# Pooling mixer, first channel group: pool the normed input before the modulation, scale afterwards, add the shift times a pooled row of ones

## The chip, the cores and the metric

The kernel runs on one core of one Trainium2 chip. The metric is the device time of one execution in microseconds (us); each figure is the median of several executions. The core has a matrix engine (TensorE, PE in the rows), a vector engine (VectorE, DVE), an activation engine (ScalarE, ACT), a general engine (GpSimd, POOL), and a queue (SyncE, SP) from which all loads of this kernel are issued. Each engine takes its instructions in the order in which the built program lists them.

## The reference, cut to what matters

Two layers of a diffusion trunk. In layer 0 the token mixer is a centred average pool over time, in four channel groups of 512 channels with windows 2, 4, 8 and 16, followed by a 512x512 product per group. It is computed for a latent stream of 256 tokens and a context stream of 256 tokens.

```python
a_lat = modulate(rms_norm(h, norm1_g[i]), ml[:, 0], ml[:, 1])   # x * (1 + scale) + shift
...
cs = jnp.cumsum(jnp.pad(ug, ((0, 0), (left + 1, right), (0, 0))), axis=1)
window_sum = cs[:, win:win + T] - cs[:, :T]
parts.append(window_sum / count[None, :, None] - ug)            # pooled minus itself
...
y = jnp.einsum('btgc,gcd->btgd', p, w).reshape(B, T, D) + b
h = h + ml[:, 2] * y_lat
```

The shift and the scale are one number per channel and come out of `silu(c) @ w_mod`. Pooling runs over time, so a scale per channel can be put on before or after it, and a shift per channel contributes the shift times what pooling makes of a row of ones.

## The kernel before, in words

Channels lie on the 128 partitions, and the two streams lie beside each other in the free axis, so a channel block of 128 is a 128x512 tile (s = 0 latent, s = 1 context). The residual is kept as `hl` and `hc`.

- `mod_pe(0, ch, ...)` (L187) computes 512 of the 12288 modulation numbers: 4 MB of `w_mod` in eight loads `wm` of 512 KB, 16 products on a quarter of the array each (L193, tile `mod`), a copy out of PSUM on ACT (L198, `modev`), four transposes on PE (L203, `modt`), and a few tiny DVE instructions that leave `modT`. It yields four times. Numbers 0 to 3 are the shift for the four groups, 4 to 7 the scale, 8 to 11 the gate, 12 to 15 the next shift, 16 to 19 the next scale. `mods()` lists them, and `need(n)` runs that list up to step n.
- `mixer(g)` (L413) handles one channel group in steps between yields. For each of its four channel blocks DVE multiplies the residual by scale and norm (`py`, L426), ACT adds the shift into a padded tile (`pad`, L428), DVE adds the window (`ws`, L434), POOL multiplies by one over the count (`pf`, L439), DVE takes off the input (L440), and `pf` is split into a high and a low part (`ph`, L442 on ACT, L443 on DVE), since a 32-bit product is done as three products. The weights `wp` are split alike (`wp0h` on ACT L142, `wp0l` on DVE L144). Then 48 products (`pm`, L457 to L459) go into four PSUM banks one after the other, each bank is read by ACT with the gate (`pz`, L464), added to the residual on POOL (L466) and squared for the next norm (`n2q`, L249). At last the updated residual times the next scale is split into `Ad` (L475, L476).
- `partial(g, ...)` multiplies `Ad` with the first blocks of the feed-forward weights (`wcg`, `wcu` split by L142 and L144; products `cg`, `cu`, L518 to L520), while the modulation loads go on.

The text of the program is not the order that runs: the builder schedules the instructions by a model of its own and fixes an order per engine. `lend` names the tiles of a pool that loads may use as room besides six of their own, so it sets how many loads can be ahead: 18 tiles of 512 KB in the first stretch.

Of the kernel before, what the change touches and what calls it, by code (L numbers as in the profile page):

```python
# [17 lines left out]
P = 128  # L18
D = 2048
KT = D // P  # L20
T = 256
# [36 lines left out]
def kernel(ctx: ExitStack, tc: tile.TileContext, xT, cxT, wmod, wg, wu, wd, wp,  # L58
# [237 lines left out]
    with ExitStack() as ph0:  # L296
# [62 lines left out]
        with ExitStack() as phs:  # L359
# [32 lines left out]
            def mods():  # L392

                for g in range(4):
                    for w in (0, 1, 2, 4):
                        yield from mod_pe(0, 4 * w + g, sc, f0)
                    yield from mod_pe(0, 12 + g, sc, f0)
                    shifts(g)
# [13 lines left out]

            def mixer(g):  # L413
# [7 lines left out]
                for i in range(4):  # L421
# [7 lines left out]
                    src, w = pad, 1  # L429
                    while w < win:  # L430
                        n = WP - 2 * w + 1
                        if w == 1:
                            dst = st.tile([P, 2, WP], F32, tag="ws", name=f"ws{k}")
                        nc.vector.tensor_tensor(dst[:, :, :n], src[:, :, :n], src[:, :, w : w + n], op=ALU.add)  # L434
                        src, w = dst, 2 * w
                    o = PAD - win // 2
                    pf = f0.tile([P, 2, T], F32, tag="t2", name=f"pf{k}")
                    for s in both:
                        nc.gpsimd.tensor_tensor(pf[:, s, :], src[:, s, o : o + T], inv_t, op=ALU.mult)  # L439
                    nc.vector.tensor_tensor(pf, pf, pad[:, :, PAD : PAD + T], op=ALU.subtract)  # L440
                    ph = ap0.tile([P, 2, 2, T], F32R, tag=f"A{k}", name=f"ph{k}")
                    nc.scalar.copy(ph[:, 0], pf)  # L442
                    nc.vector.tensor_tensor(ph[:, 1], pf, ph[:, 0].bitcast(F32), op=ALU.subtract)  # L443
                    pa.append(ph)
# [6 lines left out]
                for m in range(4):  # L451
                    ps = bank("d", f"pm{g}_{m}")
                    for i in range(4):
                        hi, lo = parts[i // 2]
                        c = 512 * (i % 2) + P * m
                        rh, rl = flat(pa[i][:, 0]), flat(pa[i][:, 1])
                        nc.tensor.matmul(ps, hi[:, c : c + P], rh, start=(i == 0), stop=False)  # L457
                        nc.tensor.matmul(ps, hi[:, c : c + P], rl, start=False, stop=False)
                        nc.tensor.matmul(ps, lo[:, c : c + P], rh, start=False, stop=(i == 3))  # L459
# [83 lines left out]
            lend(range(4, KT))  # L543
# [635 lines left out]
```

## Time and profile before

| | |
|---|---|
| median of 3 runs | 3152.26 us (3151.38 to 3156.24) |
| the profiled execution | 3144.81 us, of which the span of the instructions is 3143.0 us |
| PE busy | 3047.0 us of the span |
| DVE, ACT, POOL busy | 2034.4, 1366.9, 938.9 us |
| first product of the mixer | 57.32 us after the span's start |
| first product of the feed-forward part | 79.08 us |

Times in the rows below count from the span's start. A row of the timeline gives start, duration, engine, line of the code, operation, the tile written and the tiles read, shapes and how many instructions it merges; in brackets stands how long the engine was idle before it and who ended the wait. Matmul durations overlap, so what one costs is the distance of the starts.

### The profile page before, as it was taken

What the parts mean: (1) busy time and instruction counts of PE and PEld (TensorE: products, weight loads), DVE (VectorE), ACT (ScalarE), POOL (GpSimd) and SP (SyncE); (2) the same over time, 40 slices, a digit from 0 to 9 for tenths busy, and PEclk for the clock granted to TensorE, in tenths of its full rate; (3) what the DMA queues carried; (4) which work ended last, traced back from release to release, by engine and by line L of the source; (5) the groups of instructions that cost most, each with busy time, mean ns of one, the idle gap of its engine ahead of it and who ended that gap; (6) DMA issues with size and microseconds to landing.
All of it is one profiled execution on the core that took longest, in us unless ns stands there. A gap on an engine that the chain in (4) does not pass through costs nothing.

```text
span 3143.0 us, 40920 instructions
## 1 busy us (share of the span) xinstructions
PE 3047.0 (97%) x15082; PEld 2415.6 (77%) x15082; DVE 2034.4 (65%) x2854; ACT 1366.9 (43%) x2219; POOL 938.9 (30%) x845
## 2 busy tenths in 40 slices
PE   6999999999999999999999999999999999999998
PEld 2565568887877778787778787878778888888887
DVE  4345664387586776868676665564767666666666
ACT  4333454323233232333334444343545665556665
POOL 2011213304132140403223000000002476667776
PEclk9999999999999999999999999999999999999999
DMA  9878663375554646556463333333345555555553
GB/s 380 332 269 315 207 210 101 105 231 182 171 195 158 203 160 198 182 174 195 163 214 115 101 115 105 104 110 97 111 146 183 174 183 201 187 185 179 180 187 116
DMA packets 161545, 559.72 MB, mean 178 GB/s; under 512 B 17600, under 2 KB 22208, under 8 KB 161344
## 3 DMA queue, kind: packets, MB, share of 16 engines
q1 hardware_dynamic: 161344, 557.10, 53.1%
q8 instruction: 119, 1.95, 0.2%
q14 instruction: 82, 0.67, 0.1%
HBM read 554.93 MB, written 2.10 MB: 177 GB/s over the span
## 4 chain that ended last, share of the span: by engine, by line
PE 73%; DVE 11%; DMA 9%; issue 3%; POOL 2%; ACT 1%; SPq 0%; DVEq 0%; POOLq 0%; ACTq 0%
DMA wm<-wmod 9%; DVE macc L221 6%; PE g L731 5%; PE u L731 5%; PE d L776 4%; PE mod L193 3%; PE d L627 3%; PE d L625 3%; PE d L626 3%; PE g L732 3%; PE u L732 2%; PE d L777 2%; PE u L602 2%; PE u L603 2%; PE u L601 2%
## 5 line engine op out<-in xcount | busy, mean ns | idle before, releaser
L221 DVE SCALAR_TENSOR_TENSOR macc<-wm,sc,macc 128x512 f32<-128x512 f32 x480 | 411.0, 880 | 222.8 <-DMA wm<-wmod 218.3
L638 POOL TENSOR_TENSOR hl<-hl,dy 128x256 f32<-128x256 f32 x160 | 160.2, 1001 | 937.3 <-ACT dy L637 936.3
L788 POOL TENSOR_TENSOR hl<-hl,dy 128x256 f32<-128x256 f32 x320 | 320.3, 1034 | 45.4 <-ACT dy L786 43.8
L637 ACT ACTIVATE dy<-d,modT 128x256 f32<-128x256 f32 x320 | 133.3, 470 | 172.9 <-PE d L627 167.3
L638 POOL TENSOR_TENSOR hc<-hc,dy 128x256 f32<-128x256 f32 x160 | 180.0, 1125 | 0.0
L193 PE MATMUL mod<-wm,sc 128*32 128x512 f32 x768 | 133.8, 619 | 24.4 <-DMA wm<-wmod 24.4
L344 ACT ACTIVATE sg<-g 128x512 f32<-128x512 f32 x43 | 27.2, 631 | 295.3 <-DVE g L341 295.3
L875 POOL TENSOR_TENSOR rk<-rk,rp 128x256 f32<-128x256 f32 x16 | 13.8, 862 | 366.1 <-DVE rk L874 302.4
L786 ACT ACTIVATE dy<-d,modT 128x512 f32<-128x512 f32 x160 | 103.6, 686 | 29.7 <-PE d L777 28.3
L439 POOL TENSOR_TENSOR pf<-ws,inv 128x256 f32<-128x256 f32 x32 | 28.4, 907 | 220.4 <-DVE ws L434 152.1
L144 DVE TENSOR_TENSOR wd_2l<-wd,wd_2h 128x1024 fp32r<-128x1024 f32 (+1 forms) x44 | 57.0, 1301 | 48.4 <-ACT wd_2h L142 47.6
L755 DVE TENSOR_TENSOR actb<-sgb,actb 128x256 fp32r<-128x256 f32 x43 | 71.9, 1671 | 21.5 <-ACT actb L754 20.3
L193 PEld LDWEIGHTS mod<-wm,sc 128*32 128x32 f32 x768 | 23.5, 110 | 78.7 <-issue 61.5
L627 PE MATMUL d<-act,wd_0l 128*128 128x512 f32 x172 | 71.1, 414 | 12.3 <-DVE wd_0l L144 12.3
L144 DVE TENSOR_TENSOR wd_0l<-wd,wd_0h 128x1024 fp32r<-128x1024 f32 (+1 forms) x44 | 54.2, 1234 | 34.3 <-ACT wd_0h L142 33.6
L142 ACT CAST wd_0h<-wd 128x1024 fp32r<-128x1024 f32 (+1 forms) x44 | 45.2, 1031 | 67.5 <-PE g L602 36.1
L961 ACT ACTIVATE sb<-sb,nm 128x512 f32<-128x512 f32 x64 | 46.2, 722 | 63.1 <-DVE nm L957 61.4
L625 PE MATMUL d<-act,wd_0h 128*128 128x512 f32 x172 | 70.1, 408 | 0.0
L626 PE MATMUL d<-act,wd_0h 128*128 128x512 f32 x172 | 69.8, 406 | 0.0
L627 PE MATMUL d<-act,wd_1l 128*128 128x512 f32 x172 | 68.0, 396 | 0.1
L626 PE MATMUL d<-act,wd_2h 128*128 128x512 f32 x172 | 68.0, 395 | 0.0
L625 PE MATMUL d<-act,wd_3h 128*128 128x512 f32 x172 | 68.0, 395 | 0.0
(1754 smaller groups left out, 10054.0 us busy)
## 6 DMA issues: line engine op xcount, KB each, us to landing
wm<-wmod SPq DMA_DIRECT2D x384, 512.0 KB, 5.1
wd<-wd SPq DMA_DIRECT2D x168, 512.0 KB, 4.5
wg<-wg SPq DMA_DIRECT2D x156, 512.0 KB, 4.1
wu<-wu SPq DMA_DIRECT2D x156, 512.0 KB, 4.8
wv<-wv SPq DMA_DIRECT2D x32, 512.0 KB, 3.8
wk<-wq SPq DMA_DIRECT2D x32, 512.0 KB, 3.7
wq<-wq SPq DMA_DIRECT2D x32, 512.0 KB, 3.7
wo<-wo SPq DMA_DIRECT2D x32, 512.0 KB, 3.7
```

Of the source, the lines that this page charges most:

```text
L144: eng.tensor_tensor(lo[:, :n], t[:, :n], hi[:, :n].bitcast(F32), op=ALU.subtract)
L193: nc.tensor.matmul(ps[32 * j : 32 * j + 32, :], sc[:, 4 * g + j, :], ts[j // 2][0][:, 512 * (j % 2) : 512 * (j % 2) + 512], start=(g == 0) ...
L221: nc.vector.scalar_tensor_tensor(acc[s], w, sc2[:, k, s : s + 1], acc[s], op0=ALU.mult, op1=ALU.add)
L625: nc.tensor.matmul(ps, hi[:, o : o + P], xh, start=(i == 0), stop=False)
L626: nc.tensor.matmul(ps, hi[:, o : o + P], xl, start=False, stop=False)
L627: nc.tensor.matmul(ps, lo[:, o : o + P], xh, start=False, stop=(i == n - 1))
L637: nc.scalar.activation(y[:, s], ps[:, T * s : T * s + T], AF.Copy, scale=M(0, 5, k, s))
L638: nc.gpsimd.tensor_tensor(h_of(s)[:, k, :], h_of(s)[:, k, :], y[:, s], op=ALU.add)
L731: nc.tensor.matmul(ps, hi[:, c : c + P], flat(B[k]), start=(k == 0), stop=False)
L732: nc.tensor.matmul(ps[:, T:], lo[:, c : c + P], B[k][:, 0], start=False, stop=(k == KT - 1))
L776: nc.tensor.matmul(ps, hi[:, o : o + P], flat(acts[i]), start=(i == 0), stop=False)
L788: nc.gpsimd.tensor_tensor(hl[:, k, :], hl[:, k, :], y[:, q], op=ALU.add)
```

## The change

For group 0 alone, `mixer` works in another order. It multiplies the residual by the norm only (L468, on DVE) into the padded tiles, pools these (`windows`, `pooled`), and keeps the four results `pf` in a room of the pool that loads used before. A row `z` is made from ones in the same way. When the modulation is there, ACT scales each `pf` in place (L478), DVE adds shift times `z` (L479), and the split follows. The weights `wp0` are asked for after eight instead of eleven modulation steps, the scale is computed before the shift, the 48 products run with the channel block outside and the four banks inside (all four banks open at once), and loads have 15 rooms in the first stretch instead of 18. Groups 1 to 3 keep their instructions.

```diff
@@ mods()
-                    for w in (0, 1, 2, 4):
+                    for w in (0, 1, 2, 4) if g else (1, 0, 2, 4):
                         yield from mod_pe(0, 4 * w + g, sc, f0)
@@
+            def windows(pad, win, name):
...
+            def pooled(pf, pad, inv_t, win, name):
+                src, o = windows(pad, win, name)
+                for s in both:
+                    nc.gpsimd.tensor_tensor(pf[:, s, :], src[:, s, o : o + T], inv_t, op=ALU.mult)
+                nc.vector.tensor_tensor(pf, pf, pad[:, :, PAD : PAD + T], op=ALU.subtract)
@@ mixer(g)
+                if g == 0:
+                    z = ap0.tile([P, 1024], F32, tag="A6", name="z")[:, 0:T]
+                    one = pads[1][:, 0:1]
+                    nc.gpsimd.memset(one[:, :, PAD : PAD + T], 1.0)
+                    src, o = windows(one, win, "wz")
+                    nc.vector.tensor_tensor(z, src[:, 0, o : o + T], inv_t, op=ALU.mult)
+                    nc.vector.tensor_scalar(z, z, -1.0, None, op0=ALU.add)
+                    pfs = []
+                    for k in range(4):
...
+                        for s in both:
+                            nc.vector.tensor_tensor(pad[:, s, PAD : PAD + T], h_of(s)[:, k, :], rs1[:, T * s : T * s + T],
+                                                    op=ALU.mult)
+                        pfs.append(room[:, k % 2])
+                        pooled(pfs[k], pad, inv_t, win, f"ws{k}")
+                    yield
+                    parts = ld(wp[0], "wp0")
+                    yield
+                    for k in range(4):
+                        for s in both:
+                            v = pfs[k][:, s, :]
+                            nc.scalar.activation(v, v, AF.Copy, scale=M(0, 1, k, s))
+                            nc.vector.scalar_tensor_tensor(v, z, M(0, 0, k, s), v, op0=ALU.mult, op1=ALU.add)
+                        pa.append(parts_of(pfs[k], k))
+                    yield
+                    banks = [bank("gu", f"pm0_{m}") for m in range(4)]
+                    for i in range(4):
+                        for m in range(4):
+                            pool_mm(banks[m], parts, pa, i, m)
@@ the driver
-            lend(range(4, KT))
+            lend(range(7, KT))
             mix = mixer(0)
-            for n in STEPS:
-                need(n + 2)
+            for n in (0, 8, 11, 15, 15, 19, 19):
+                need(n)
                 next(mix)
```

The built orders show what the scheduler makes of it. First ACT, after the copy of the first norm (`rs`). Before, from there to the first split of a pooled block; `modev_0` and `modev_4` are the shift and the scale of group 0:

```order
L369 COPY rs_194<-n1b 128x512
L198 COPY modev_0_239<-mod_0_206 128x512
L198 COPY modev_4_282<-mod_4_249 128x512
L428 ACTIVATE pad_198<-py_322,modT_0_246 128x256 x2
L428 ACTIVATE pad_200<-py_336,modT_0_246 128x256 x2
L442 CAST ph_333<-pf_329 128x512
```

Now, the same stretch of ACT:

```order
L369 COPY rs_194<-n1b 128x512
L198 COPY modev_4_279<-mod_4_246 128x512
L478 ACTIVATE pf_216<-pf_216,modT_4_286 128x256 x4
L478 ACTIVATE pf_231<-pf_231,modT_4_286 128x256 x4
L198 COPY modev_0_323<-mod_0_290 128x512
L142 CAST wp0h_329<-wp_0_325 128x1024
L142 CAST wp0h_333<-wp_1024_327 128x1024
L433 CAST ph_374<-pf_216 128x512
```

The second modulation copy now stands behind the scaling of all four pooled blocks, and the weight split stands behind that copy.

Second, PE around the mixer's first products. Before, the modulation products of number 8 stand together, ahead of the mixer:

```order
L193 MATMUL mod_8_293<-wm_8_2_0_310,sc 32x512 x2
L193 MATMUL mod_8_293<-wm_8_2_1024_312,sc 32x512 x2
L193 MATMUL mod_8_293<-wm_8_3_0_390,sc 32x512 x2
L193 MATMUL mod_8_293<-wm_8_3_1024_392,sc 32x512 x2
L203 MATMUL modt_8_400<-ident,modev_8_398 128x128 x4
L193 MATMUL mod_16_408<-wm_16_0_0_409,sc 32x512 x2
L457 MATMUL pm_0_435<-ph_333,wp0h_382 128x512
```

Now, the middle of the mixer's products:

```order
L442 MATMUL pm_1_442<-ph_381,wp0h_329 128x512
L193 MATMUL mod_8_345<-wm_8_2_0_362,sc 32x512 x2
L443 MATMUL pm_1_442<-ph_381,wp0l_330 128x512
L442 MATMUL pm_2_443<-ph_381,wp0h_329 128x512
L443 MATMUL pm_2_443<-ph_381,wp0l_330 128x512
L442 MATMUL pm_3_444<-ph_381,wp0h_329 128x512
L443 MATMUL pm_3_444<-ph_381,wp0l_330 128x512
L193 MATMUL mod_8_345<-wm_8_2_1024_364,sc 32x512 x2
L441 MATMUL pm_0_441<-ph_388,wp0h_333 128x512
```

The last four loads of number 8 are now multiplied one by one between mixer products, and the transposes `modt_8` stand behind all 48 of these.

Third, ACT from the last bank of group 0 to the first feed-forward weights. Before:

```order
L464 ACTIVATE pz_514<-pm_3_501,gbi_321,gsc_320 128x256 x2
L249 ACTIVATE n2q_519<-hl 128x256
L198 COPY modev_16_531<-mod_16_408 128x512
L249 ACTIVATE n2q_519<-hc 128x256
L142 CAST wcg_0h_591<-wcg_0_0_587 128x1024
L475 ACTIVATE Ad_567<-hl,modT_16_538 128x256
L475 ACTIVATE Ad_567<-hc,modT_16_538 128x256
```

Now:

```order
L514 ACTIVATE pz_522<-pm_3_444,gbi_209,gsc_208 128x256 x2
L249 ACTIVATE n2q_518<-hc 128x256
L249 ACTIVATE n2q_527<-hl 128x256
L198 COPY modev_16_539<-mod_16_416 128x512
L249 ACTIVATE n2q_527<-hc 128x256
L525 ACTIVATE Ad_575<-hl,modT_16_546 128x256
...
L525 ACTIVATE Ad_590<-hc,modT_16_546 128x256
L142 CAST wcg_0h_599<-wcg_0_0_595 128x1024
```

The split of the first feed-forward weights moved from ahead of the eight `Ad` to behind them.

## Rows read from the trace of the kernel before

**Rows 1.** First part of the page: busy time, share of the span, instructions.
```profile
PE 3047.0 (97%) x15082; PEld 2415.6 (77%) x15082; DVE 2034.4 (65%) x2854; ACT 1366.9 (43%) x2219; POOL 938.9 (30%) x845
```

**Rows 2.** Busy time by stretch: engines in turn, granted clock, DMA share, GB/s.
```profile
40.00:60.00 20.00, 13.54 (x56) 4.38 (x57) 16.31 (x29) 9.03 (x16) 6.72 (x8) 0.91 1.03 408
60.00:80.00 20.00, 18.55 (x98) 9.11 (x97) 6.62 (x14) 11.31 (x25) 5.69 (x8) 1.00 1.00 385
...
51.00:55.00 4.00, 2.85 (x8) 0.18 (x4) 4.00 (x6) 2.74 (x5) 1.54 (x2) 0.57 1.03 409
...
80.00:220.00 140.00, 139.90 (x786) 84.24 (x785) 52.60 (x93) 48.16 (x82) 12.91 (x16) 1.00 0.83 300
220.00:436.00 216.00, 214.31 (x1145) 123.66 (x1144) 148.19 (x258) 93.73 (x174) 48.67 (x45) 1.00 0.77 268
```

**Rows 3.** Timeline of PE, from the second modulation to the feed-forward products.
```profile
40.38 0.66 PE L203 MATMUL modt<-ident,modev 128*128 128x128 f32 x4 [0.69 <-ACT modev L198]
...
50.65 3.20 PE L193 MATMUL mod<-wm,sc 128*32 128x512 f32 x8 [2.79 <-DMA wm<-wmod]
...
72.73 0.39 PE L458 MATMUL pm<-ph,wp0h 128*128 128x512 f32 x1
72.95 0.39 PE L459 MATMUL pm<-ph,wp0l 128*128 128x512 f32 x1
...
79.08 0.73 PE L518 MATMUL cg<-Ad,wcg_0h 128*128 128x512 f32 x2
```

**Rows 4.** Timeline of PE: modulation products in a row, and alone between others.
```profile
76.37 2.78 PE L193 MATMUL mod<-wm,sc 128*32 128x512 f32 x24
...
80.81 0.39 PE L518 MATMUL cg<-Ad,wcg_0h 128*128 128x512 f32 x1
81.13 1.05 PE L193 MATMUL mod<-wm,sc 128*32 128x512 f32 x4
...
82.45 0.39 PE L520 MATMUL cg<-Ad,wcg_0l 128*128 128x512 f32 x1
```

**Rows 5.** Timeline of ACT in the first 80 us.
```profile
31.30 0.59 ACT L369 COPY rs<-n1b 128x512 f32<-128x512 f32 x1 [11.01 <-PE n1b L272]
...
39.74 0.59 ACT L198 COPY modev<-mod 128x512 f32<-128x512 f32 x1 [6.80 <-PE mod L193]
42.36 0.91 ACT L428 ACTIVATE pad<-py,modT 128x256 f32<-128x256 f32 x2 [2.03 <-DVE py L426]
...
52.54 1.03 ACT L142 CAST wp0h<-wp 128x1024 fp32r<-128x1024 f32 x1
...
64.41 1.02 ACT L464 ACTIVATE pz<-pm,gbi,gsc 128x256 f32<-128x256 f32 x2 [5.00 <-PE pm L459]
65.81 0.42 ACT L249 ACTIVATE n2q<-hl 128x256 f32<-128x256 f32 x1 [0.38 <-POOL hl L466]
...
77.31 0.51 ACT L475 ACTIVATE Ad<-hl,modT 128x256 fp32r<-128x256 f32 x1 [0.33 <-DVE modT L183]
77.73 0.49 ACT L475 ACTIVATE Ad<-hc,modT 128x256 fp32r<-128x256 f32 x1
```

**Rows 6.** Timeline of DVE in the first 80 us.
```profile
43.30 0.72 DVE L434 TENSOR_TENSOR ws<-pad 128x542 f32<-128x542 f32 x1 [0.64 <-ACT pad L428]
...
45.73 0.69 DVE L440 TENSOR_TENSOR pf<-pf,pad 128x512 f32<-128x512 f32 x1 [0.53 <-POOL pf L439]
...
52.74 1.22 DVE L144 TENSOR_TENSOR wp0l<-wp,wp0h 128x1024 fp32r<-128x1024 f32 x1
...
78.33 0.48 DVE L476 SCALAR_TENSOR_TENSOR Ad<-hl,modT,Ad 128x256 fp32r<-128x256 f32 x1
78.73 0.48 DVE L476 SCALAR_TENSOR_TENSOR Ad<-hc,modT,Ad 128x256 fp32r<-128x256 f32 x1
```

**Rows 7.** Timeline of POOL in the first 80 us.
```profile
44.16 1.54 POOL L439 TENSOR_TENSOR pf<-ws,inv 128x256 f32<-128x256 f32 x2 [16.49 <-DVE ws L434]
47.20 1.80 POOL L439 TENSOR_TENSOR pf<-ws,inv 128x256 f32<-128x256 f32 x2 [1.50 <-DVE ws L434]
```

More of the change, by code (lines that the diff above doesn't have):

```diff
@@ L411, with parts_of, pool_mm @@
             STEPS = (9, 9, 9, 9, 13, 13, 17, 17)
+            def windows(pad, win, name):
+                src, w = pad, 1
+                while w < win:
+                    n = WP - 2 * w + 1
+                    if w == 1:
+                        dst = st.tile([P, 2, WP], F32, tag="ws", name=name)[:, 0 : pad.shape[1]]
+                    nc.vector.tensor_tensor(dst[:, :, :n], src[:, :, :n], src[:, :, w : w + n], op=ALU.add)
+                    src, w = dst, 2 * w
+                return src, PAD - win // 2
+            def pooled(pf, pad, inv_t, win, name):
[3 more added lines that the diff above has]
+                nc.vector.tensor_tensor(pf, pf, pad[:, :, PAD : PAD + T], op=ALU.subtract)
+            def parts_of(pf, k):
+                ph = ap0.tile([P, 2, 2, T], F32R, tag=f"A{k}", name=f"ph{k}")
+                nc.scalar.copy(ph[:, 0], pf)
+                nc.vector.tensor_tensor(ph[:, 1], pf, ph[:, 0].bitcast(F32), op=ALU.subtract)
+                return ph
+            def pool_mm(ps, parts, pa, i, m):
+                hi, lo = parts[i // 2]
+                c = 512 * (i % 2) + P * m
+                rh, rl = flat(pa[i][:, 0]), flat(pa[i][:, 1])
+                nc.tensor.matmul(ps, hi[:, c : c + P], rh, start=(i == 0), stop=False)
+                nc.tensor.matmul(ps, hi[:, c : c + P], rl, start=False, stop=False)
+                nc.tensor.matmul(ps, lo[:, c : c + P], rh, start=False, stop=(i == 3))
             def mixer(g):
@@ L420, in mixer @@
                 pa = []
-                for i in range(4):
+                banks = []
+                if g == 0:
[7 more added lines that the diff above has]
+                    for k in range(4):
+                        if k % 2 == 0:
+                            room = ap0.tile([P, 2, 2, T], F32, tag=f"A{4 + k // 2}", name=f"pf{k}")
+                        pad = pads[k % 2]
+                        for s in both:
[17 more added lines that the diff above has]
+                            pool_mm(banks[m], parts, pa, i, m)
+                for i in range(4 if g else 0):
                     k = 4 * g + i
@@ L428, in mixer @@
                         nc.scalar.activation(pad[:, s, PAD : PAD + T], y[:, s], AF.Identity, bias=M(0, 0, k, s))
[L429 to L436, printed above, removed]
-                    pf = f0.tile([P, 2, T], F32, tag="t2", name=f"pf{k}")
[L438 to L444, printed above, removed]
+                    pf = f0.tile([P, 2, T], F32, tag="t2", name=f"pf{k}")
+                    pooled(pf, pad, inv_t, win, f"ws{k}")
+                    pa.append(parts_of(pf, k))
                     if i == 3:
@@ L451, in mixer @@
                 for m in range(4):
[L452 to L459, printed above, removed]
+                    if banks:
+                        ps = banks[m]
+                    else:
+                        ps = bank("d", f"pm{g}_{m}")
+                        for i in range(4):
+                            pool_mm(ps, parts, pa, i, m)
                     k = 4 * g + m
```

## The prediction

> **What bounds the kernel now.** I read the page's busy times first: PE is busy for 97% of the span [rows 1], so a change can win only where PE waits, and loses wherever it gives PE more to do. Then the stretches around the first mixer group [rows 2]. From 40 to 60 us PE is busy for 13.54 us and from 60 to 80 us for 18.55 us, so it waits 7.9 us in all; the loads run at 408 and 385 GB/s meanwhile, at full share. From 80 us on there is nothing left to win: 139.90 us busy of 140, then 214.31 of 216. So whatever the change does has to show in the instant at which the first feed-forward product starts, 79.08 us [rows 3], and in the PE work behind it. Last the timeline of PE [rows 3]: one wait of 2.79 us at 50.65 us is for a load, and the products behind it take 3.20 us because the granted clock is down (0.57 on average from 51 to 55 us [rows 2], which is the lower level, 1.2 GHz, for most of it). That cost 0.43 x 4 = 1.7 us of full speed. The most that the edit can win on the way to 79.08 us is thus 7.9 + 1.7 = 9.6 us, 0.3% of the time. About 0.2%, 6.3 us, is what a measurement of this kernel can tell from no change.
>
> **The change, first part: the way to the first feed-forward product.** I follow the new orders with durations from the rows; the clock of the trace of before is the scale.
>
> 1. The copy of the first norm ends at 31.30 + 0.59 = 31.9 us [rows 5]. Now 128 KB of counts are loaded ahead of the weights (0.3 us at 408 GB/s) and two small instructions for the row of ones stand in DVE's chain ahead of the norm. I add 0.4 us: 32.3.
> 2. DVE's four multiplies at 0.40 us a start (the nearest row is the `Ad` pair, 78.33 to 78.73 [rows 6]) and a window addition of 0.7 [rows 6]: 34.6. POOL then needs 1.54 to 1.80 us for a block [rows 7], say 1.65: 36.3 for the first, 38.0 for the second. The two padded tiles are used twice, so the third block waits for the subtraction from the second (0.65, as DVE's 0.69 row overlaps a little [rows 6]) and its own window addition: POOL runs it from 39.4 to 41.1 and the fourth to 42.8; its subtraction ends at 43.5.
> 3. ACT scales the fourth block in two instructions, 0.9 [rows 5]: 44.4. Only then may it copy the shift out of PSUM, which before began at 39.74 [rows 5]: it ends at 45.0 instead of 40.3. PE's transposes (0.66 [rows 3]) stand next on PE, so PE waits for them, and they end at 45.7.
> 4. ACT's two weight splits stand behind that copy (1.03 each [rows 5]): 46.0 and 47.0. DVE takes the first low part (1.22 [rows 6]) to 47.2, the tiny shift instructions to 47.6, the second low part to 48.7, eight additions of shift times row at 0.40 to 51.95, the first low part of a block to 52.6. The first mixer products (high parts) run at about 50, seven us earlier than the 57.3 us of before.
> 5. From 52.6 on PE is the pace. 44 of the 48 products are left, at 0.228 each (72.73 to 72.95 [rows 3]): 10.0. Four lone modulation loads stand among them. Of these one costs 1.64 - 2 x 0.228 = 1.18 us (80.81 to 82.45 with one product and the run between [rows 4]), against 2.78 for six loads in a row, or three pairs [rows 4]: 4.7. That is 67.3. The clock may be low at this point, as after the wait at 50.65; I take half of the 1.7 us: 68.2.
> 6. Now the part that overlapped before: the four banks finish together, and the gate's transposes stand behind all 48 products. Transposes 0.6 and four tiny DVE instructions: 69.7. From the read of a bank to the square of its residual 1.4 us go by (64.41 to 65.81 [rows 5]), and the next bank's read stands behind that square (0.34 more), so a bank takes 1.74 and four take 7.0: 76.7. Then the copy of number 16 (0.6), its transposes (0.65), DVE (0.6): 78.55. In the meantime PE has nothing but four more pairs of loads, and waits some 4 us.
> 7. Eight `Ad` on ACT at 0.41 a start [rows 5]: 81.9. The split of the first feed-forward weights stands behind them now: high part 82.9, low part 84.1. Four products go ahead of the low part (0.9), so PE is where it would be with a start at 83.2.
>
> Before, that start was 79.08. The first part costs **4.1 us**: pooling does begin earlier, but ACT's order holds back the shift, and the evictions that lay under products before lie bare. The unknown prices: the multiply of residual by norm has no row, between 0.35 (DVE's additions, scaled by their length) and 0.48 each; the clock term between 0 and 1.7 for one gap, with up to three gaps (at 46, 52 and 73 to 77 us); POOL between 1.54 and 1.80. Together -2 to +4 us around the 4.1.
>
> The rooms: load n now waits for the release of load n - 15. By the release times above the 42nd load, the second half of the first feed-forward weights, can be issued at about 70 us and is needed after 84; cover of more than 10 us, so nothing for it, and 1 us if that cover were gone. The scratch instructions on DVE and POOL before 31 us are in step 1. Memsets lie in the first 5 us, where DVE and POOL have no other work.
>
> **Second part: modulation products between others.** The scheduler, set off by another start, arranges the rest of the head anew. Counted in PE's order from the first feed-forward product to the last modulation product, the 308 modulation products stand in 76 runs before and in 83 now. A run costs 0.86 us for each four products begun (76.37 to 79.08 for 24 instructions, which are twelve products: 2.71 = 3 x 0.86 + 0.13 [rows 3, 4]) and 0.32 us for going in and out (1.18 - 0.86). The begun fours grow from 102 to 106. So PE gets 7 x 0.32 + 4 x 0.86 = **5.6 us** more work, in a stretch in which it waited 1.8 us of 356 [rows 2]. Bounds: nothing, if the new arrangement fills waits that I don't see; 7, if the new crossings to the short transposes cost as much.
>
> The other engines: DVE is busy 52.60 of 140 and 148.19 of 216 us there [rows 2], and gets nothing new; the later groups keep their instructions.
>
> **The sum.** 4.1 + 5.6 = 9.7 us. The profiled execution took 3144.81 us and would take 3154.5. The median is 7.5 us above that execution, so on the median: 3152.3 + 9.7 = **3162.0 us**, +0.31%.
>
> **The rivals.**
> - *Only the first part counts.* The seven extra runs fill waits of PE. For it: schedulers place loose work where they see a wait. Against it: 1.8 us of waits in 356 us [rows 2]. It gives 3152.3 + 4.1 = 3156.4 us, no change that can be told.
> - *The waits of PE are filled, and it isn't slower.* Pooled blocks are ready when the shift comes, so PE goes through 40 to 79 us without a wait. For it: the long chain from modulation to first product, 40.4 to 57.3 us, is just what the edit takes apart. Against it: the three places of ACT's order above. Its price is the whole 9.6 us, so with the second part 3152.3 - 9.6 + 5.6 = 3148.3. It decides as soon as the first feed-forward product comes before 79.8 us, since then first and second part stay under 6.3 us together.
> - *The clock falls and stays low.* The new order has three gaps of 3 to 5 us on PE before 80 us, where before had one of 2.79 us that lowered the clock [rows 2, 3]. If each costs the full 1.7 us on the path, the sum grows by 3 x 1.7 - 0.85 = 4.2 us: 3166 us. The Trainium skill, in "TensorE: Matmul & The Clock Gate", part 1 on the clock gate, has the half clock as the state to which the array goes back whenever it has been idle for a while, and which only sustained work ends; by it every one of the three gaps would be paid for. The trace agrees at its one gap (0.57 granted).
>
> **How the numbers follow.** Both parts as summed: 0.5. Only the first part: 0.2. The waits filled: 0.2. The clock: 0.1. The first is the forecast, 3162 us. The range must take in the cases on both sides: from 3150, which keeps the upper part of the case with filled waits, to 3168, a little above the clock's case. Within the first case alone it is 3157 to 3166. Slower by over 0.2%: most of the first and all of the last, 0.57. Faster by over 0.2% needs filled waits and a second part near nothing: 0.06. The same: 0.37.
>
> **What would show it.** In the profile after: the copy of the shift at about 44 us, behind the scaling; first mixer products near 50, the last near 68; a PE wait of 4 us between 70 and 78; the first feed-forward product at 83. Then PE busy without a wait to 440 us, with the last modulation product some 10 us later than before. The prediction is wrong if pooling is done before 40 us, if the evictions overlap, or if the modulation products between 80 and 440 us take no more PE time than before.

## The result, and the profile after

Over 20 executions each, the changed kernel took a median of 3159.95 us (3152.95 to 3169.00) and the kernel before 3150.62 us (3142.39 to 3156.24). The ratio is 1.0032, with a 95% interval of 1.0023 to 1.0040: 9.3 us slower, where 9.7 were forecast. The forecast of 3162.0 us lies 2.0 us above the measured median; 1.6 of these are the baseline, since the prediction had the median of three executions of the kernel before (3152.26) and this is the median of 20. The profiled execution of the changed kernel took 3169.00 us, the longest of its 20, over a span of 3167.2 us. So 24 us between the two profiles is more than the change did; which part of it belongs to the change is read below from places in the program.

First the page's busy times:

```profile
PE 3058.2 (97%) x15082; PEld 2419.7 (76%) x15082; DVE 2031.6 (64%) x2865; ACT 1364.5 (43%) x2219; POOL 940.3 (30%) x846
```

Then the same stretches as in [rows 2] (busy time and count of PE, PEld, DVE, ACT, POOL, then granted clock, DMA share, GB/s):

```profile
40.00:60.00 20.00, 12.67 (x47) 6.22 (x48) 10.81 (x20) 6.65 (x11) 2.38 (x3) 0.66 1.03 408
60.00:80.00 20.00, 14.93 (x82) 7.06 (x85) 4.08 (x9) 7.81 (x18) 6.63 (x8) 0.97 0.86 305
80.00:100.00 20.00, 17.98 (x105) 9.12 (x97) 7.71 (x17) 8.48 (x15) 0.00 (x0) 0.95 0.95 335
100.00:220.00 120.00, 120.00 (x658) 70.14 (x662) 47.42 (x83) 41.12 (x72) 13.12 (x16) 1.00 0.80 292
220.00:436.00 216.00, 213.31 (x1134) 123.66 (x1127) 135.62 (x239) 85.53 (x160) 42.10 (x43) 0.99 0.73 254
```

PE has as many instructions as in [rows 1] and is busy for 11.2 us more. In the first two stretches it is busy for 0.87 and 3.62 us less than in [rows 2], so it waits 12.4 us there where it waited 7.9. The waits did not go; they grew.

The timeline of PE shows the places. In the changed kernel L441 to L443 are the mixer's products, and L568 to L570 are the first feed-forward products:

```profile
45.22 1.12 PE L203 MATMUL modt<-ident,modev 128*128 128x128 f32 x4 [5.78 <-ACT modev L198]
46.27 1.94 PE L193 MATMUL mod<-wm,sc 128*32 128x512 f32 x8
50.31 2.07 PE L441 MATMUL pm<-ph,wp0h 128*128 128x512 f32 x4 [2.11 <-ACT ph L433]
52.32 1.94 PE L193 MATMUL mod<-wm,sc 128*32 128x512 f32 x8
54.18 0.74 PE L442 MATMUL pm<-ph,wp0h 128*128 128x512 f32 x1
...
56.36 1.07 PE L441 MATMUL pm<-ph,wp0h 128*128 128x512 f32 x4
...
57.72 0.39 PE L442 MATMUL pm<-ph,wp0h 128*128 128x512 f32 x1
58.04 1.05 PE L193 MATMUL mod<-wm,sc 128*32 128x512 f32 x4
59.02 0.50 PE L443 MATMUL pm<-ph,wp0l 128*128 128x512 f32 x1
59.36 0.39 PE L442 MATMUL pm<-ph,wp0h 128*128 128x512 f32 x1
...
69.12 0.39 PE L443 MATMUL pm<-ph,wp0l 128*128 128x512 f32 x1
69.35 0.60 PE L203 MATMUL modt<-ident,modev 128*128 128x128 f32 x4
69.88 3.64 PE L193 MATMUL mod<-wm,sc 128*32 128x512 f32 x32
78.59 1.11 PE L203 MATMUL modt<-ident,modev 128*128 128x128 f32 x4 [5.07 <-ACT modev L198]
...
84.75 0.50 PE L568 MATMUL cg<-Ad,wcg_0h 128*128 128x512 f32 x1 [1.17 <-ACT wcg_0h L142]
```

Four waits stand there, each with ACT as the releaser: 5.78 us for the copy of the shift, 2.11 us for the first split block, 5.07 us for the copy of modulation number 16, and 1.17 us for the split of the first feed-forward weights. The mixer's first product comes 7.0 us earlier than before (50.31 against 57.32), its last one 3.8 us earlier (69.12 against 72.95 in [rows 3]), and the first feed-forward product 5.7 us later (84.75 against 79.08).

The timeline of ACT says why these copies come so late:

```profile
43.80 0.91 ACT L478 ACTIVATE pf<-pf,modT 128x256 f32<-128x256 f32 x2 [0.91 <-DVE pf L429]
44.61 0.56 ACT L198 COPY modev<-mod 128x512 f32<-128x512 f32 x1
45.07 1.99 ACT L142 CAST wp0h<-wp 128x1024 fp32r<-128x1024 f32 x2
49.64 0.62 ACT L433 CAST ph<-pf 128x512 fp32r<-128x512 f32 x1 [2.58 <-DVE pf L479]
...
70.88 1.02 ACT L514 ACTIVATE pz<-pm,gbi,gsc 128x256 f32<-128x256 f32 x2 [4.77 <-DVE gbi L502]
...
72.61 1.00 ACT L514 ACTIVATE pz<-pm,gbi,gsc 128x256 f32<-128x256 f32 x2
...
77.97 0.57 ACT L198 COPY modev<-mod 128x512 f32<-128x512 f32 x1
...
83.27 0.49 ACT L525 ACTIVATE Ad<-hc,modT 128x256 fp32r<-128x256 f32 x1
83.67 1.98 ACT L142 CAST wcg_0h<-wcg 128x1024 fp32r<-128x1024 f32 x2
```

The shift's copy stands behind the last scaling (44.61). The four bank reads begin at 70.88, behind all mixer products; the first of them waited for the gate (`gbi`, from DVE), whose transposes stand behind these products too. A bank takes 1.73 us; the next copy follows them (77.97), and the split of the feed-forward weights follows the eight `Ad` (83.67).

To compare the rest of the head between kernels I use one product that all of them have: the first one with weight block 8 (`wg_8h`), which comes a few microseconds behind the last modulation product (the landmark of the expectations below). Timelines of PE, the kernel before and then after:

```profile
439.34 0.50 PE L601 MATMUL g<-A,wg_8h 128*128 128x512 f32 x1 [0.88 <-DVE late L328]
```

```profile
455.69 0.50 PE L651 MATMUL g<-A,wg_8h 128*128 128x512 f32 x1 [0.88 <-DVE late L328]
```

From the first feed-forward product to this one, 360.3 us went by before and 370.9 after. Of the latter 2.6 us are waits for loads, where a second execution of the same kernel has 0.5. Behind the longest of them, which ended at 391.50, the granted clock was 0.50 from 392.6 to 396.1 us, worth 1.7 us of full speed; the second execution has no such fall there:

```profile
391.50 1.05 PE L193 MATMUL mod<-wm,sc 128*32 128x512 f32 x4 [1.92 <-DMA wm<-wmod]
```

### The profile page after: what moved, and what is told of

Same layout as the page of the kernel before. It is cut to its first block, busy times and chain, and to the rows that moved or that the text cites. A ratio compares the mean times of both kernels' runs of the same rounds, so it can differ in the third digit from the quotient of the medians.

```text
span 3167.2 us, 40924 instructions
## 1 busy us (share of the span) xinstructions
PE 3058.2 (97%) x15082; PEld 2419.7 (76%) x15082; DVE 2031.6 (64%) x2865; ACT 1364.5 (43%) x2219; POOL 940.3 (30%) x846
## 4 chain that ended last, share of the span: by engine, by line
PE 69%; DMA 13%; DVE 11%; issue 3%; POOL 3%; ACT 1%; SPq 0%; DVEq 0%; POOLq 0%; ACTq 0%
DMA wm<-wmod 12%; DVE macc L221 5%; PE g L781 5%; PE u L781 4%; PE d L826 4%; PE d L677 3%; PE mod L193 3%; PE d L675 3%; PE d L676 3%; PE g L782 2%; PE u L782 2%; PE d L827 2%; PE k L951 2%; PE q L969 2%; PE k L953 2%
## 5 line engine op out<-in xcount | busy, mean ns | idle before, releaser
L344 ACT ACTIVATE sg<-g 128x512 f32<-128x512 f32 x43 | 27.2, 632 | 309.3 <-DVE g L341 309.3
L925 POOL TENSOR_TENSOR rk<-rk,rp 128x256 f32<-128x256 f32 x16 | 13.8, 861 | 366.0 <-DVE rk L924 302.4
```

## The experiments

All of them by the same three places, in us. Each row is one profiled execution, whose time stands under "this execution"; the last column has the medians of the timed runs against the kernel before on the same chip, where there are any. "To block 8" counts from the first feed-forward product to the product above, "the rest" from there to the span's end.

| kernel | first mixer product | first feed-forward product | to block 8 | the rest | this execution | ratio of the timed runs, 95% |
|---|---|---|---|---|---|---|
| before | 57.3 | 79.1 | 360.3 | 2703.7 | 3144.81 | |
| b1_before_again | 58.2 | 81.2 | 360.3 | 2703.7 | 3147.02 | |
| after | 50.3 | 84.8 | 370.9 | 2711.5 | 3169.00 | 1.0032 (1.0023 to 1.0040) |
| a1_after_again | 49.4 | 83.4 | 367.9 | 2700.9 | 3154.04 | |
| rooms15 | 57.7 | 80.1 | 362.6 | 2701.8 | 3146.35 | 1.0010 (1.0000 to 1.0020) |
| rooms18 | 47.1 | 82.4 | 364.5 | 2702.6 | 3151.18 | 1.0026 (1.0017 to 1.0035) |
| scale_dve | 45.7 | 80.6 | 367.7 | 2714.5 | 3164.60 | 1.0045 (1.0029 to 1.0062) |
| no_shift_term | 47.5 | 84.8 | 366.0 | 2709.7 | 3162.33 | |
| bank_turn | 53.3 | 79.9 | 361.6 | 2706.8 | 3150.05 | 1.0010 (1.0000 to 1.0019) |
| bank_turn18 | 55.3 | 80.7 | 358.5 | 2698.0 | 3139.01 | 0.9990 (0.9979 to 1.0000) |
| no_shift_mod | 52.1 | 73.7 | 339.0 | 2708.5 | 3122.98 | 0.9925 (0.9910 to 0.9940) |
| early_no_shift | 50.2 | 76.0 | 343.8 | 2713.2 | 3134.83 | 0.9934 (0.9920 to 0.9948) |

The theory: the loss has two parts, of which the first lies ahead of the first feed-forward product (ACT holds back the shift, and the bank reads lie bare), and the second lies in modulation products that the new arrangement scatters among others. The rivals: only one of the parts is real, or the clock is the cause.

**Both kernels once more, on one chip.**

> The kernel before, unchanged, for a second trace. Landmark: the first product of weight block 8 (end of the head), 439.3 us in the first trace of before. If the head is fixed by the order of instructions, it comes at 439 to 440 again, and the executions differ only behind it. If the head itself varies from execution to execution, it comes more than 2 us elsewhere.

> The changed kernel, unchanged, for a second trace. In its first trace the landmark came at 455.7 us, 16.4 later than before, while the medians differ by 9.3. Theory 1 (the head varies): it comes nearer to 449 to 451 this time, since two waits for loads and a fall of the clock between 350 and 400 us in the first trace are not there each time. Theory 2 (the head is fixed and some of its loss is won back later): 455 to 456 again.

Rows of PE, the kernel before and then the changed one:

```profile
81.24 0.73 PE L518 MATMUL cg<-Ad,wcg_0h 128*128 128x512 f32 x2
...
441.50 0.50 PE L601 MATMUL g<-A,wg_8h 128*128 128x512 f32 x1 [0.88 <-DVE late L328]
```

```profile
83.44 0.50 PE L568 MATMUL cg<-Ad,wcg_0h 128*128 128x512 f32 x1
...
451.36 0.50 PE L651 MATMUL g<-A,wg_8h 128*128 128x512 f32 x1 [0.88 <-DVE late L328]
```

Measured: block 8 came at 441.5 us and at 451.4 us, 9.9 us apart. Of these, 81.2 to 83.4 us is 2.2 for the first part, and 360.3 to 367.9 us is 7.7 for the second. So a difference of the size of the timed runs' 9.3 us is there in the head alone, and the 8 us by which the first profile of after is longer behind block 8 is not there in this pair (2703.7 and 2700.9 us). The first part varies from pair to pair: 5.7 us between the two first profiles, 2.2 here. The kernel before moved by 2.2 us itself: the granted clock stayed at 0.50 from 51 to 61 us in this execution, through its first mixer products, and from 51.2 to 54.6 in the first.

**The rooms alone, and the change with all its rooms.** rooms15 is the kernel before with 15 rooms for loads:

```diff
-            lend(range(4, KT))
+            lend(range(7, KT))
```

rooms18 is the changed kernel with the pooled blocks and the row of ones in tiles of their own, so that loads keep 18 rooms:

```diff
-                    z = ap0.tile([P, 1024], F32, tag="A6", name="z")[:, 0:T]
+                    z = act_tile("z", F32)[:, 0, 0:T]
-                            room = ap0.tile([P, 2, 2, T], F32, tag=f"A{4 + k // 2}", name=f"pf{k}")
+                            room = act_tile(f"pf{k}", F32).rearrange("p k (s t) -> p k s t", s=2)
-            lend(range(7, KT))
+            lend(range(4, KT))
```

> The kernel before with 15 rooms instead of 18 in the first stretch, nothing else. First feed-forward product as before (79 us, at most 1 later). Modulation products now in 79 runs and 103 begun fours instead of 76 and 102. Theory of two parts: 3 x 0.32 + 1 x 0.86 = 1.8 us more PE time in the head, landmark at 441, time +1 to +3 us. Rival, all of the loss lies ahead of the first feed-forward product: landmark within 0.5 us of before. Rival, fewer rooms hold back loads: waits of PE for wm appear, 3 us or more.

> The changed kernel with its scratch tiles elsewhere, so that loads have 18 rooms again. The instructions up to the first feed-forward product keep the order of the changed kernel; behind it the modulation products stand in 80 runs and 104 begun fours (83 and 106 in the changed kernel, 76 and 102 before). Theory of two parts: first feed-forward product at 84.8 as in the changed kernel, then 4 x 0.32 + 2 x 0.86 = 3.0 us more than before instead of 5.6, landmark 448 to 449, time about 2 to 3 us below the changed kernel's and 6 above before's. Rival, all of the loss lies ahead of that product: same time as the changed kernel.

Fewer rooms cost nothing on the way to the first feed-forward product (80.1, between 79.1 and 81.2), but 2.4 us behind it. Waits for loads there are 0.5 us, against 0.3 before: the scheduler, with other rooms, puts the modulation products into 79 runs with 103 begun fours instead of 76 and 102. With 18 rooms the changed kernel has 80 runs and 104 begun fours instead of 83 and 106, and takes 3.5 us less to block 8 than the second execution of that kernel. Its first feed-forward product came at 82.4 us, not at the 84.8 expected, in an execution whose first norm ended 3.2 us earlier than in after. In the timed runs the difference between rooms18 and the changed kernel (0.26% and 0.32%) is smaller than either interval.

**The banks in turn.** The changed kernel, with early pooling, scaling behind it and 15 rooms, but with the four banks multiplied one after the other, so that each is read while PE works on the next:

```diff
-                    banks = [bank("gu", f"pm0_{m}") for m in range(4)]
-                    for i in range(4):
-                        for m in range(4):
-                            pool_mm(banks[m], parts, pa, i, m)
```

> The changed kernel with the four mixer banks of group 0 multiplied one after the other, as in the other groups, instead of all four side by side; pooling, scaling and rooms stay as changed. In the built order the gate's transposes stand ahead of the mixer products again, the reads of a bank between the products of the next, and from the first feed-forward product on 77 runs and 101 begun fours (76 and 102 before). Theory of two parts: mixer products from about 54 to 72 us, the last bank is followed by 1.4 + 0.34 + 1.85 us and by eight Ad and the weight split, 4.3 us: first feed-forward product at 80 to 81 us, 2 to 4 earlier than in the changed kernel. The second part vanishes: landmark (first product of weight block 8) at 441 to 443, time within 3 us of before. Rival, the loss comes from pooling and scaling in the new order (ACT holding back the shift) and not from the banks: first feed-forward product stays at 83 to 85.

The loss is gone but for 0.10% (0 to 0.19): first feed-forward product at 79.9 us, 361.6 us from there to block 8, of which 2.6 us are waits for loads, with 77 runs and 101 begun fours. One edit takes back both parts.

**The banks in turn, and 18 rooms.** The two edits above together.

> The changed kernel with the four banks multiplied in turn and with all 18 rooms for loads. The head then has 78 runs of modulation products and 101 begun fours (before: 76 and 102). If the two parts of the loss are as stated and nothing is left of either: first feed-forward product at 79 to 81 us, first product of the eighth weight block 359 to 362 us behind it, landmark at 439 to 442 us, time within 3 us of the kernel before. If early pooling is worth something once neither part stands against it, it is 3 to 6 us faster than before, with the first feed-forward product at 73 to 77 us.

Neither part is left: 80.7 us, 358.5 us. Its timed runs are 0.10% below those of before (0 to 0.21), inside the 0.2% that can be told from no change. In this trace the bank reads lie under the products; timelines of ACT and then of PE:

```profile
58.32 1.02 ACT L510 ACTIVATE pz<-pm,gbi,gsc 128x256 f32<-128x256 f32 x2 [3.51 <-PE pm L443]
...
65.82 1.02 ACT L510 ACTIVATE pz<-pm,gbi,gsc 128x256 f32<-128x256 f32 x2 [5.00 <-PE pm L443]
...
69.82 1.02 ACT L510 ACTIVATE pz<-pm,gbi,gsc 128x256 f32<-128x256 f32 x2 [1.48 <-PE pm L443]
...
72.54 1.02 ACT L510 ACTIVATE pz<-pm,gbi,gsc 128x256 f32<-128x256 f32 x2 [0.19 <-PE pm L443]
```

```profile
45.43 1.11 PE L203 MATMUL modt<-ident,modev 128*128 128x128 f32 x4 [5.59 <-ACT modev L198]
...
55.28 0.48 PE L441 MATMUL pm<-ph,wp0h 128*128 128x512 f32 x1
...
74.89 0.66 PE L203 MATMUL modt<-ident,modev 128*128 128x128 f32 x4 [1.45 <-ACT modev L198]
```

Each bank is read as soon as its products are done, and PE waits 1.45 us before the transposes of number 16 instead of 5.07. The wait of 5.59 us for the shift is still there, and still the kernel isn't slower than before: in this order the shift's lateness costs nothing, since PE has the products and transposes of number 8 to do before the mixer (its first product is at 55.28 us). Nor does early pooling win anything once it costs nothing: the last block is pooled at 44.0 us, against 58.7 before, and PE is busy for 31.1 us from 40 to 80 us, against 32.1. PE does modulation products while the mixer's input is made in either kernel, and the same work has to be done before the first feed-forward product.

**ACT's part alone.** The scaling goes from ACT to DVE, so that the copy of the shift needn't wait for it:

```diff
-                            nc.scalar.activation(v, v, AF.Copy, scale=M(0, 1, k, s))
+                            nc.vector.tensor_scalar(v, v, M(0, 1, k, s), None, op0=ALU.mult)
```

> The changed kernel with the scaling of the pooled blocks on DVE instead of ACT, so that ACT copies the shift out of PSUM at once (about 39.5 us instead of 44.6). Everything from the first feed-forward product on keeps the order of the changed kernel (83 runs, 106 begun fours). If ACT's order alone held the first part back, the mixer's low-part products start 4 to 5 us earlier than 52.6 to 54.2 and the time falls by 4 us. By the rows DVE is next in line: its last subtraction at 43.7, scale 0.6, shift 0.4, eight additions 3.2, two weight splits 2.4, first low part 0.7 give 51.1, so 1.5 to 3 us earlier, first feed-forward product at 81 to 82.5, time 1 to 3 us below the changed kernel's.

The timeline of its ACT:

```profile
29.53 0.58 ACT L198 COPY modev<-mod 128x512 f32<-128x512 f32 x1 [0.47 <-DVE pad L468]
39.68 0.58 ACT L198 COPY modev<-mod 128x512 f32<-128x512 f32 x1 [9.56 <-PE mod L193]
...
45.02 0.62 ACT L433 CAST ph<-pf 128x512 fp32r<-128x512 f32 x1 [2.86 <-DVE pf L479]
```

The hold is gone: the shift is copied at 39.68, as soon as PE has it. But in this execution the first norm also ended 2.8 us earlier (the copy of the scale at 29.53, against 32.30 in after). Counted from that copy the first split block comes 1.9 us earlier than in after (15.5 us against 17.3), and the first feed-forward product 1.4 us earlier (51.1 against 52.5). Against the other two executions with ACT's scaling, counted the same way, it is 1.0 us (a1) and 2.0 us (rooms18, whose norm ended at about the same time as here). DVE, which now scales as well, is the next to be waited for; the 5.1 us wait before number 16 stays. The time expected, 1 to 3 us below the changed kernel's, did not come, and the total is no better than after's (0.45% above before, against 0.32%, with intervals that overlap): the way to block 8 takes 367.7 us, with the same 83 runs and 106 fours, and its trace is the longest behind block 8.

**The shift's term left out.** The row of ones and the eight additions of shift times that row (3.25 us of DVE) are taken away; the term is zero but for rounding, since pooling minus itself of a constant row is zero. The shift is still computed.

```diff
-                            nc.vector.scalar_tensor_tensor(v, z, M(0, 0, k, s), v, op0=ALU.mult, op1=ALU.add)
```

> The changed kernel without the row of pooled ones and the eight additions of shift times that row (pooling minus identity takes a constant to zero, so the term is zero but for rounding). The shift is still computed, and nothing waits for it. From the first feed-forward product on 79 runs and 103 begun fours, as in the kernel with 15 rooms. Theory of two parts: low-part products from 47.5 us, but eight lone modulation loads stand among them, so the last comes at 66 to 67 and the first feed-forward product at 81 to 82.5; from it to the landmark 362.5 us as with 15 rooms, landmark 444 to 445. Rival, the first part is set by the shift's arrival: first feed-forward product at 79 or below.

This missed. The mixer starts 2.8 us earlier (47.5), and the first feed-forward product comes at 84.8 us all the same. Two rows of its PE show the wait for the shift's copy, which nobody needs now but which still stands in PE's order, and the first product:

```profile
45.23 1.12 PE L203 MATMUL modt<-ident,modev 128*128 128x128 f32 x4 [5.69 <-ACT modev L198]
47.49 0.79 PE L441 MATMUL pm<-ph,wp0h 128*128 128x512 f32 x1 [1.15 <-ACT wp0h L142]
```

The 2.8 us went into the mixer's products: from the first to the last with high parts on both sides (L441) they take 21.2 us instead of 18.4, because the scheduler puts eight lone modulation loads among them instead of four (and one pair). Behind them the chain of bank reads is as in after (5.01 us of waiting). There is one execution of this kernel and no timed run. To block 8 it takes 366.0 us with 79 runs and 103 fours (1.4 us of it are waits for loads), where 362 follows from the prediction's prices for runs and begun fours; those prices do not hold here.

**No shift of the mixer at all, with and without early pooling.** In the first kernel the edit is to before: the products and the 16 MB of loads for the shift of the four groups are left out, which changes the result by rounding only. In the second, the same, and group 0 is pooled unmodulated and scaled afterwards, the banks in turn.

```diff
-                    for w in (0, 1, 2, 4):
+                    for w in (1, 2, 4):
...
-                    y = f0.tile([P, 2, T], F32, tag="t2", name=f"py{k}")
...
-                        nc.scalar.activation(pad[:, s, PAD : PAD + T], y[:, s], AF.Identity, bias=M(0, 0, k, s))
+                        nc.vector.scalar_tensor_tensor(pad[:, s, PAD : PAD + T], h_of(s)[:, k, :], M(0, 1, k, s),
+                                                       rs1[:, T * s : T * s + T], op0=ALU.mult, op1=ALU.mult)
```

> The kernel before, with the shift of layer 0's mixer left out in all four groups: since pooling minus identity takes a constant per channel to zero, the shift cannot reach the result. The four modulation numbers 0 to 3 are neither loaded (16 MB) nor multiplied, DVE writes the scaled input straight into the padded tile, and the step counts are adapted. From the first feed-forward product on 54 runs and 76 begun fours (76 and 102 before): by the prices of the rows 22 x 0.32 + 26 x 0.86 = 29 us less PE time there, and 4 MB less to wait for ahead of the mixer, some 8 us. If PE time in the head is what counts, the landmark comes at 400 to 408 and the time falls by 30 to 38 us. If loads or DVE bound the head, at most half of that.

> No shift of the mixer's modulation in any group (pooling minus identity of a constant is zero but for rounding, so its products and its 16 MB of loads are left out), and the first group pooled unmodulated and scaled behind pooling, with the four banks multiplied in turn: no shift term, and nothing on ACT's path that the shift has to wait behind. 57 runs and 78 begun fours against 54 and 76 of the kernel without shift and without early pooling. If early pooling itself buys something where nothing is lost by it: first feed-forward product at 68 to 71 us instead of 73.7, and 2 to 5 us faster than that kernel's 3122.5, 3117.5 to 3120.5. If the head is bound by loads there (it waited 4.1 us for them), early pooling buys nothing: first product at 73 to 76 us, 3122 to 3126 us.

Leaving the shift out wins 23.3 us (0.75%, 0.60 to 0.90) and gives the fastest kernel of this study. It wins less than expected: block 8 comes 26.7 us earlier than before, not 31 to 39, since PE now waits where less modulation work is there to fill in: 9.7 us (2.6 before) between the first feed-forward product and block 8, 4.1 of them for loads, besides the waits of the rows below. Rows of PE, this kernel and then the one with early pooling:

```profile
39.61 3.04 PE L193 MATMUL mod<-wm,sc 128*32 128x512 f32 x8 [3.14 <-DMA wm<-wmod]
47.49 1.12 PE L203 MATMUL modt<-ident,modev 128*128 128x128 f32 x4 [4.84 <-ACT modev L198]
```

```profile
49.45 1.11 PE L203 MATMUL modt<-ident,modev 128*128 128x128 f32 x4 [7.29 <-ACT modev L198]
```

With early pooling added it takes 3126.37 us (0.66% under before, 0.52 to 0.80): no gain over the kernel without. The first feed-forward product comes 2.3 us later, in an execution whose first norm ended 4.0 us later. ACT holds back the gate's copy until all four blocks are scaled and split (48.82 us), the same mechanism as with the shift; in the kernel without early pooling the copy stands behind the third split (46.86).

## Why the prediction was right

The forecast was 9.7 us and 9.3 were measured, and the traces show both parts where they were put. That the two numbers are so close is partly luck: the first part, worked out as 4.1 us, measured 5.7 and 2.2 us in the two pairs of traces and 3.4 in the mean of three traces against three; the second, worked out as 5.6, measured 7.7. The errors have opposite signs.

- **Steps 1 to 4 (pooling, scaling, the held copy, the splits).** Each came within 0.7 us of the trace up to the weight split: the last subtraction ended at 43.76 (43.5 worked out), the shift's copy began at 44.61 (44.4), its transposes ended at 46.3 (45.7). The first mixer products came at 50.31 (about 50), the first with a low part at 54.18 (52.6). That last one was late because of the clock, which stood at 0.50 there: DVE began the low parts at 51.90, as worked out (51.95), but PE still had the four products and two modulation loads ahead of it to do at the lower clock.
- **Step 5 (PE as the pace).** Four lone loads among the products, as counted, and at the price worked out: from the product ahead of the first (57.72) to the second product behind it (59.36) it is 1.64 us, less two products 1.18. The last product ended at 69.5 (69.12 + 0.39), where 68.2 was worked out; of the 1.6 us that step 4 had come out late, 1.3 were left. no_shift_term agrees that PE is the pace: a start 2.8 us earlier, but with eight lone loads on the way, gives a last product at the same time (69.21).
- **Step 6 (the bare bank reads).** 1.74 us a bank worked out, 1.73 measured (70.88 to 72.61); the wait put at 4 us was 5.07. With the banks in turn (bank_turn18) the wait falls to 1.45 us and the first feed-forward product is back at 80.7, so the first part hangs on this step; the edit also lets the scheduler put number 8 ahead of the mixer, which was not taken apart from it.
- **Step 7 and the size of the first part.** 4.1 us were worked out. The three traces in the order of before (before, b1, rooms15) have the first feed-forward product at 80.1 us in the mean, and the three with the four banks side by side and ACT's scaling (after, a1, rooms18) at 83.5: 3.4 us, and in after 0.2 more for the low part of the weights. The prediction named ACT's hold on the shift and the bank reads side by side, without a price for each; scale_dve puts the hold at 1.0 to 2.0 us with the banks side by side, and in bank_turn18 it costs nothing.
- **The second part.** 5.6 us were worked out from 7 more runs and 4 more begun fours (the terms add up to 5.7), and 7.7 were measured. Added up from the distances of starts in PE's timeline without the waits, before against a1: modulation products 96.3 to 101.7 us (5.4 more), feed-forward products 190.3 to 190.7 (0.4 more), mixer products of the later groups 33.1 to 34.2 (1.0 more), the small products `pwg` and `pwu` 16.5 to 18.0 (1.5 more), transposes 0.4 less, waits 0.5 less. The price of a run, 0.32 us, was read from a product ahead of a lone load and one behind it, which take 0.32 and 0.34 us to the next instead of 0.23. So it already holds what the neighbours pay, and the term has to be set against the first three numbers: 6.9 us where 5.7 were priced. What the prediction had no term for are the small products, 1.5 us. Over the kernels with the shift's modulation more runs mean a longer way on the whole (76 to 78 runs: 358.5 to 361.6 us; 79: 362.6 and 366.0; 80: 364.5; 83: 367.7 to 370.9), but the price of a single run is not settled by them.
- **The rooms.** They were costed at nothing, since no load would be late. Hardly one was (0.5 us of waits), and yet the one trace with 15 rooms in the old kernel took 2.4 us longer to block 8; the timed runs show 0.10% (0 to 0.20). The place where this cost belongs is the second part: the rooms too set off another arrangement.
- **The rivals.** *Only the first part*: fell, 7.7 us lie behind the first feed-forward product. *The waits are filled*: fell, they grew from 7.9 to 12.4 us. Its own condition, the first feed-forward product before 79.8 us, was nearly met by bank_turn (79.9), and that kernel's loss is 0.10%. *The clock*: the windows of one microsecond in the profile after show how much of it came true:

```profile
41.00:42.00 1.00, 0.00 (x0) 0.00 (x0) 0.94 (x2) 0.03 (x1) 0.58 (x1) 0.54 1.03 410
42.00:43.00 1.00, 0.00 (x0) 0.00 (x0) 0.00 (x0) 0.88 (x2) 1.00 (x2) 0.50 1.04 414
...
53.00:54.00 1.00, 1.00 (x8) 0.00 (x0) 1.00 (x3) 0.00 (x0) 0.00 (x0) 0.50 1.09 422
54.00:55.00 1.00, 1.00 (x7) 0.70 (x4) 0.40 (x1) 0.00 (x0) 0.00 (x0) 0.64 1.03 401
55.00:56.00 1.00, 1.00 (x6) 0.83 (x5) 0.00 (x0) 0.00 (x0) 0.00 (x0) 1.00 1.01 399
```

The clock was at its lower level of 1.2 GHz from 42 to 54 us: it fell in the wait before 45.22 and rose only in the products behind 50.31. But in most of that time PE had nothing to do or was about to wait anyway. On the path lie the four first products (2.01 us to the next start, against 0.91 at 56.36) and the two modulation loads behind them (1.86): they put the first product with a low part at 54.18, 1.6 us after DVE had ended the first low part (52.59). That product itself took 0.35 more (0.58 to the next start against 0.23). The third gap brought the clock down as well (0.50 from 79 to 82 us); there only the transposes at 78.59 lie on the path (1.11 us against 0.60 at 69.35), 0.5 us more. Together it is some 2.4 us; the rival had 5.1. Its price of 1.7 us a gap was too high from the start: 0.43 x 4 us counts the whole stretch from 51 to 55 us, in which PE was busy for 2.85 us [rows 2]. The rule of the Trainium skill ("TensorE: Matmul & The Clock Gate", part 1) that idleness takes the clock back and sustained work ends it agrees with these rows; that every gap would be paid for in full does not come true here, since a low clock ahead of another wait costs nothing.

What stays open is the rest, from block 8 on. It takes 2698 to 2714.5 us in these executions, and the two profiles of the same changed kernel differ by 10.6 us there. The timed medians average over it; single profiles don't. I have no cause for it. Whether the longer first part is the reason for the other arrangement, or the order of the products by itself, wasn't separated either: bank_turn takes back both at once.

## What to carry to other kernels

An earlier start of a chain wins only if the waiting engine had nothing else to do: here PE had loose modulation work to do either way, and having the last block pooled 14.8 us sooner (44.0 against 58.7 us) bought nothing even where it cost nothing. Before opening several PSUM banks side by side, look at what reads them: finished together, four reads of 1.73 us lay bare that had lain under products. Where a scheduler fixes the order, count the runs of short loose products in the built order as well as the waits: in the second pair of traces the scattering of the same 308 products cost more (7.7 us) than the longer waits ahead of them (2.2).

## What the runs showed of the hardware that was not expected

- **A low clock can last over two waits.** In after the 5.78 us and the 2.11 us waits had four transposes and eight modulation instructions between them (45.22 to 48.2), and the granted clock stayed at 0.50 right through these. In b1_before_again, with the order of before, it was 0.50 from 51 to 61 us, through work that took 8.0 of these 10 us, where the first profile of before had 0.50 from 51.2 to 54.6. So the same order pays for a low clock by different amounts from one execution to the next.
- **The first products run at the lower clock, for a time that differs between executions, and the profile shows 1.00 there.** The first norm's copy `rs` starts at 27.2 to 28.5 us in five of the twelve executions and at 30.3 to 31.5 in seven, whichever kernel it is (before 31.30, rooms15 with the same start of the program 27.19). PE shows where it comes from; in after and then in rooms18, whose first products start at the same 19.29 us:

```profile
25.82 3.64 PE L193 MATMUL mod<-wm,sc 128*32 128x512 f32 x16
```

```profile
24.31 2.34 PE L193 MATMUL mod<-wm,sc 128*32 128x512 f32 x16
```

The 16 small products for the norm (`n1s`) just ahead of these took 3.57 us in after and 2.05 in rooms18. One modulation product of a quarter of the array lasts 1.06 us in after until 29 us and 0.62 or 0.59 from 31.1 on; 1.06 is also what it lasts at the granted clock of 0.50 (before, 51.9 us). The trace's record of the granted clock begins at 30.8 us in after and at 22.6 in rooms18, just where the products become fast, and the profile's view by stretch counts time without a record as full: that is why it gives 1.00 from 19 to 31 us for both. In all twelve traces the record begins at 21.5 to 23.3 us where the norm is early and at 28.7 to 30.8 where it is late. Why it differs isn't shown. In the old kernel the earlier norm did not bring the first feed-forward product forward (rooms15, 80.1); PE waited 2.80 us for a load at 49.56 there.
